# Moving one of two modulation blocks of each mixer from VectorE to TensorE in a two-layer decoder trunk

## The chip, the cores and the metric

The kernel runs on one core of one Trainium2 chip. Its engines are TensorE (PE, with its weight loads as PEld), VectorE (DVE), ScalarE (ACT), GpSimd (POOL) and SyncE (SP, which here issues most DMAs). The metric is the device time of one execution in microseconds (us), lower is better; a kernel's time is the median of its runs.

## What is computed

The reference is a trunk of two layers over 256 tokens of width 1024, in float32. Each layer has a token mixer (attention heads and RWKV-7 heads side by side) and a feed-forward part, both with adaptive modulation from one condition vector `c`:

```python
cond = jax.nn.silu(c)
for l in range(DEPTH):
    mod = cond @ w_ada[l] + b_ada[l]                       # 1024 x 6144
    sh1, sc1, gt1, sh2, sc2, gt2 = split(mod, 6)
    h = rms_norm(x, g_norm_mix[l]) * (1 + sc1) + sh1
    proj = h @ w_cat
    y_mla = mla_mixer(proj[..., :MLA_COLS], ...)           # 4 attention heads
    y_rwkv, v_first = rwkv7_mixer(token_shift(...), ...)   # 8 heads, state recurrence
    x = x + gt1 * (concat(y_mla, y_rwkv) @ w_out[l])
    h = rms_norm(x, g_norm_ffn[l]) * (1 + sc2) + sh2
    f = swiglu(...) if l % 2 == 0 else moe_swiglu(...)
    x = x + gt2 * f
return rms_norm(x, g_final)
```

The product `cond @ w_ada[l]` has one row, so each weight is used once. Its 6144 columns are cut into three blocks of 2048: block 0 holds sh1 and sc1, block 1 gt1 and sh2, block 2 sc2 and gt2.

## The kernel before

The program runs start, mixer 0, dense feed-forward 0, mixer 1, and a mixture of experts (MoE) that streams 8 experts' weights. Products that need full precision are split into high and low halves: ACT casts the high half (`split`, L187), DVE subtracts for the low one (L189), and `products` (L169) issues three matmuls per weight tile.

A mixer is written as seven threads that take turns by weights (`TUNE`, `run`): `projections` (w_in, L169 into `pp`), `prepare`, the two `recurrence` threads, `attention`, `output`, and `side`. A scheduler then sets the order on each engine, so what a thread issues lands between the instructions of the others, and each engine runs its own queue strictly in order. The recurrence inverts triangular tiles by doubling: TensorE multiplies 32x32 tiles (L716), ACT copies (`Wd`, L734), TensorE multiplies again, DVE merges (L738) and transposes (`Xd`, L743), and round again.

`side` computes blocks 1 and 2 of the layer by `ada_block`, while block 0 is done earlier (at the start for layer 0, in the feed-forward part of layer 0 for layer 1). `ada_block` loads eight weight tiles `raw` of 128x2048 from a ring of five tiles that it shares with `project` and `wout`, and has two ways to use a tile, by its argument `on_pe`:

```python
if on_pe:
    ps = ps or psp.tile([P, 512], F32, name="ada", tag="ada", bufs=1)
    for g in range(4):
        nc.tensor.matmul(ps[32 * g:32 * g + 32, :], condr[:, k, :],
                         raw[:, g * 512:(g + 1) * 512], start=k == 0, stop=k == KD - 1)
    yield
    continue
acc = acc or raw
for g in range(0, 2048, 1024):
    ...
        behind(nc.vector.tensor_scalar(acc[:, gs], raw[:, gs], ccol[:, k:k + 1], None, op0=OP.mult), first)
    ...
        nc.vector.scalar_tensor_tensor(acc[:, gs], raw[:, gs], ccol[:, k:k + 1], acc[:, gs], ...)
    yield
```

On TensorE (L233) the stationary operand is the condition repeated over 32 columns, and the four quarters of a tile go to four column groups of the array, which fill the four 32-partition parts of one PSUM bank. On DVE (L242 for the first tile, L244 for the other seven) a tile takes two instructions of 128x1024, the first tile is kept as the sum, and four matmuls with a matrix of ones (L250) add the 128 partitions at the end. Then in both ways DVE adds the bias (`ms`, L256), and four transposes (L260) and a copy (L261) put the columns into `modT`. POOL issues the load of the bias `bb` (L224), which has one buffer.

In the profile an f32 matmul counts as two instructions, so a set of four column groups is "x8".

Of the kernel before, what the change touches and what calls it, by code (L numbers as in the profile page):

```python
# [105 lines left out]
def tile_trunk(ctx: ExitStack, tc: tile.TileContext, a, out, fo, mo):  # L106
# [11 lines left out]
    def bank(name="ps", bufs=None, dt=F32):  # L118
        return psp.tile([P, 512], dt, name=name, tag="ps", bufs=bufs)
# [45 lines left out]
    def raw_tile():  # L165
        return rawp.tile([P, 2048], F32, name="raw", tag="raw")
# [12 lines left out]
    def behind(op, first):  # L179

        if first is not None:
            tc.add_manual_dep(op.ins, first.ins.name, NOSYNC, reason="order")
# [13 lines left out]
    def columns(l):  # L196
        pt = bank("pt")
        nc.tensor.transpose(pt[:, :NROWS], prow[l], ident[:NROWS, :NROWS])
        pc = cst.tile([P, NROWS], F32, name=f"par{l}")
        nc.vector.tensor_copy(pc, pt[:, :NROWS])  # L200
        par.append({k: pc[:, o:o + n] for k, (o, n) in ROWS.items()})
        omu = cst.tile([P, 15], F32, name=f"omu{l}")
        nc.vector.tensor_scalar(omu, par[l]["mu"], -1.0, 1.0, op0=OP.mult, op1=OP.add)
        oka = cst.tile([P, 4], F32, name=f"oka{l}")
        nc.vector.tensor_scalar(oka, par[l]["ka"], -1.0, 1.0, op0=OP.mult, op1=OP.add)
        par[l]["omu"], par[l]["oka"] = omu, oka
# [13 lines left out]
    def ada_block(l, blk, on_pe=False, raw_tile=raw_tile, first=None):  # L220

        ba = a["b_ada"]
        bb = mid.tile([P, 512], F32, name="bb", tag="bb", bufs=1)
        nc.gpsimd.dma_start(bb, bass.AP(tensor=ba.tensor, offset=ba.offset + l * 6 * D + blk * 2048,  # L224
                                        ap=[[512, 4], [0, 32], [1, 512]]))
        ps = acc = None
        for k in range(KD):
            raw = raw_tile()
            sync.dma_start(raw, a["w_ada"][l, k * P:(k + 1) * P, blk * 2048:(blk + 1) * 2048])
# [10 lines that stand above are left out]
                gs = slice(g, g + 1024)  # L240
                if k == 0:
                    behind(nc.vector.tensor_scalar(acc[:, gs], raw[:, gs], ccol[:, k:k + 1], None, op0=OP.mult), first)  # L242
                else:
                    nc.vector.scalar_tensor_tensor(acc[:, gs], raw[:, gs], ccol[:, k:k + 1], acc[:, gs],  # L244
                                                   op0=OP.mult, op1=OP.add)
                yield
        if not on_pe:
            ps = psp.tile([P, 512], F32, name="ada", tag="ada", bufs=1)
            for g in range(4):
                nc.tensor.matmul(ps[32 * g:32 * g + 32, :], ones[:, 0:32], acc[:, g * 512:(g + 1) * 512],  # L250
                                 start=True, stop=True)
        if (l, blk) == (1, 2):
            ms = cst.tile([P, 512], F32, name=f"ms1{blk}")
        else:
            ms = mid.tile([P, 512], F32, name="ms", tag="ms", bufs=2)
        nc.vector.tensor_add(ms, ps, bb)  # L256
        yield
        pt = bank("pt")
        for q in range(4):
            nc.tensor.transpose(pt[:, q * P:(q + 1) * P], ms[:, q * P:(q + 1) * P], ident)  # L260
        nc.vector.tensor_copy(modT[l][:, blk * 16:(blk + 1) * 16].rearrange("p (g q) -> p q g", g=4),  # L261
                              pt.rearrange("p (q n) -> p q n", q=4)[:, :, 0:P:32])
        rows[l, blk] = ms
# [128 lines left out]
    mark = {}  # L392

    def mixer(l, side, branch=()):
        pr, tune = par[l], TUNE[l]
        mp = ctx2.enter_context(tc.tile_pool(name=f"mix{l}", bufs=1, reuse_waits="tile"))
# [627 lines left out]
        def output():  # L1024
# [27 lines left out]
            for n in range(2):  # L1052
                for q, z in ((0, zh), (1, zh), (0, zl)):
                    for k in range(4):
                        mm(acc[1][n], ws[k][q][:, cs[n]], z[:, k, :], False, z is zl and k == 3, False)

        threads = dict(p=projections(), w=prepare(), r=recurrence(0), s=recurrence(1), a=attention(), o=output(), x=side(need))
        run(*[(threads[k], tune[k]) for k in tune["order"]])
        return zv["acc"], zv["gates"]


    def dense_ffn(l, side, mix):
        fd = ctx2.enter_context(tc.tile_pool(name="ffndown", bufs=1, reuse_waits="tile"))
        fp = ctx2.enter_context(tc.tile_pool(name="ffn", bufs=1, reuse_waits="tile"))
# [536 lines left out]
    for l in range(2):  # L1601
        with ExitStack() as ctx2:
            def side(need):
                yield from need(TUNE[l]["side"])
                for blk in (1, 2):
                    yield from ada_block(l, blk, first=mark.get("level4"))
                if l == 0:
                    columns(1)

            acc = mixer(l, side, acc or ())  # L1610
        with ExitStack() as ctx2:
            if l == 0:
                acc = dense_ffn(l, [(1, 0)], acc)
            else:
                midctx.close()
                moe(l, acc)
# [33 lines left out]
```

## Time and profile before

| | us |
|---|---|
| median of 3 runs | 1554.27 |
| lowest and highest run | 1550.27, 1559.34 |
| the profiled execution | 1553.52 |
| its span, first to last instruction | 1551.6 |
| PE busy | 1457.0 (94%) |
| DVE busy | 564.0 (36%) |
| ACT busy | 343.9 (22%) |
| POOL busy | 141.2 (9%) |
| mean granted TensorE clock | 0.976 |

Mixer 0 lies at about 33 to 246 us of the span and mixer 1 at about 438 to 660 us; the rest is the start, the dense feed-forward part between them, and the experts. A profile's windows give the busy time of each engine in a stretch, and the TensorE clock that was granted there as a share of 2.4 GHz. In a timeline row the two first numbers are the start and the busy time in us; what stands in brackets is the idle time of the engine before it and what ended it ("issue": nothing that the profile shows).

### The profile page before, as it was taken

Reading aid. Unit: us, or ns where it says so; the run is one execution under the profiler, and the core shown is the slowest. Engines: PE = TensorE matmul, PEld = TensorE weight load, DVE = VectorE, ACT = ScalarE, POOL = GpSimd, SP = SyncE. Lnnn points to the kernel's source line nnn. Section 1 sums busy time; section 2 is a strip of 40 time slices with the busy share of each in tenths; the row PEclk is TensorE's granted clock in tenths of the full one; section 3 lists DMA queues with packets and bytes.
Section 4 is the critical chain, followed back from the end, with each engine's and each line's share of the span. In section 5 each row is a group of like instructions: output and inputs, shape, how many; then the busy total and the mean of one; then the engine's idle time right before and its main releaser. Section 6 shows DMA issues by size and latency. Waiting matters only on the chain. (4 is left out here: it accounts for less than half of the span.)

```text
span 1551.6 us, 38224 instructions
## 1 busy us (share of the span) xinstructions
PE 1457.0 (94%) x16941; PEld 911.3 (59%) x16941; DVE 564.0 (36%) x1080; ACT 343.9 (22%) x709; POOL 141.2 (9%) x188
## 2 busy tenths in 40 slices
PE   5988998999989899999999999999999999999885
PEld 1976787999969668844535535444354454444432
DVE  1699868765567996721002002020010010000001
ACT  2823326444456243220000001000000000010001
POOL 1224100000043520100000000000000000000020
PEclk9999999999989798999999999999999999999998
DMA  9836526844545454468997999999999999999994
GB/s 321 279 116 245 184 98 242 330 188 151 181 139 178 173 209 168 149 281 329 416 414 294 415 414 412 418 413 412 418 412 388 415 413 413 415 413 417 414 411 186
DMA packets 114598, 476.51 MB, mean 307 GB/s; under 512 B 14735, under 2 KB 23707, under 8 KB 91900
## 3 DMA queue, kind: packets, MB, share of 16 engines
q1 hardware_dynamic: 111932, 469.96, 77.7%
q0 software_dynamic: 2496, 4.05, 0.9%
q8 instruction: 135, 2.21, 0.6%
q14 instruction: 35, 0.29, 0.0%
HBM read 472.92 MB, written 1.05 MB: 305 GB/s over the span
## 5 line engine op out<-in xcount | busy, mean ns | idle before, releaser
L1368 PE MATMUL up<-rawx,g 128*32 128x512 f32 (+1 forms) x2120 | 205.8, 542 | 3.5 <-DMA rawx<-in_w_exp_up_dram 3.3
L1378 DVE TENSOR_TENSOR sg<-sg,up 128x512 f32<-128x512 f32 (+1 forms) x42 | 26.1, 621 | 502.7 <-PE up L1368 501.6
L1368 PE MATMUL up<-raw,g 128*32 128x384 f32 (+1 forms) x1784 | 171.5, 537 | 1.6 <-DMA raw<-in_w_exp_up_dram 1.6
L1368 PEld LDWEIGHTS up<-rawx,g 128*32 128x32 f32 x2120 | 68.0, 110 | 135.4 <-issue 115.4
L1368 PEld LDWEIGHTS up<-raw,g 128*32 128x32 f32 x1784 | 57.5, 110 | 110.9 <-issue 100.2
L1368 PE MATMUL up<-rawt,g 128*32 128x512 f32 (+1 forms) x1120 | 109.7, 540 | 1.2 <-DMA rawt<-in_w_exp_up_dram 1.2
L189 DVE TENSOR_TENSOR wlo<-raw,whi 128x512 fp32r<-128x512 f32 x140 | 97.0, 729 | 32.4 <-PE ps L169 18.1
L1402 PE MATMUL acc<-rawx,hid 128*32 128x256 f32 x1792 | 100.2, 379 | 4.9 <-DMA rawx<-in_w_exp_down_dram 4.9
L1402 PE MATMUL acc<-raw,hid 128*32 128x256 f32 x1648 | 92.5, 380 | 2.4 <-DMA raw<-in_w_exp_down_dram 2.4
L187 ACT CAST whi<-raw 128x512 fp32r<-128x512 f32 x140 | 80.2, 624 | 59.0 <-PE ps L169 26.8
L169 PE MATMUL ps<-hh,whi 128*128 128x256 f32 x352 | 87.8, 287 | 1.8 <-ACT hh L187 1.8
L169 PE MATMUL ps<-hl,whi 128*128 128x256 f32 x352 | 87.9, 286 | 0.1
L1390 ACT COPY hid<-pt 128x512 f32<-128x512 f32 (+1 forms) x26 | 13.9, 533 | 328.8 <-PE pt L1389 328.2
L169 PE MATMUL pp<-hh,whi 128*128 128x256 f32 x296 | 80.0, 305 | 6.3 <-ACT hh L187 3.5
L1402 PEld LDWEIGHTS acc<-rawx,hid 128*32 128x32 f32 x1792 | 57.5, 110 | 45.7 <-issue 5.0
L1377 ACT ACTIVATE sg<-up 128x512 f32<-128x512 f32 (+1 forms) x42 | 22.9, 544 | 254.1 <-PE up L1368 254.1
L1443 POOL TENSOR_TENSOR fa<-fa,gate 128x512 f32<-128x512 f32 x4 | 5.1, 1281 | 814.0 <-ACT gate L272 814.0
L169 PE MATMUL pp<-hl,whi 128*128 128x256 f32 x296 | 76.8, 294 | 0.5 <-DVE hl L189 0.2
L1368 PEld LDWEIGHTS up<-rawt,g 128*32 128x32 f32 x1120 | 36.2, 110 | 68.7 <-issue 61.0
L1402 PEld LDWEIGHTS acc<-raw,hid 128*32 128x32 f32 x1648 | 52.5, 110 | 39.9 <-DMA raw<-in_w_exp_down_dram 4.3
L244 DVE SCALAR_TENSOR_TENSOR raw<-raw,ccol 128x1024 f32<-128x1024 f32 x56 | 75.0, 1359 | 0.1
L169 PEld LDWEIGHTS ps<-hh,whi 128*128 128x128 f32 x352 | 68.4, 195 | 3.7 <-ACT hh L187 2.2
(448 smaller groups left out, 2218.3 us busy)
## 6 DMA issues: line engine op xcount, KB each, us to landing
rawx<-in_w_exp_down_dram SPq DMA_DIRECT2D x43, 1024.0 KB, 17.7
raw<-in_w_ada_dram SPq DMA_DIRECT2D x40, 1024.0 KB, 5.0
raw<-in_w_exp_down_dram SPq DMA_DIRECT2D x39, 1024.0 KB, 13.3
rawx<-in_w_exp_up_dram SPq DMA_DIRECT2D x38, 1024.0 KB, 19.8
rawt<-in_w_exp_gate_dram SPq DMA_DIRECT2D x23, 1024.0 KB, 15.8
raw<-in_w_exp_gate_dram SPq DMA_DIRECT2D x30, 768.0 KB, 17.4
rawt<-in_w_exp_down_dram SPq DMA_DIRECT2D x22, 1024.0 KB, 18.4
raw<-in_w_exp_up_dram SPq DMA_DIRECT2D x21, 1024.0 KB, 16.1
```

The source lines that it names most:

```text
L169: nc.tensor.matmul(ps, w if left else x, x if left else w, start=start, stop=stop)
L187: c = nc.scalar.copy(hi, src)
L189: v = nc.vector.tensor_sub(lo, src, hi.bitcast(F32))
L244: nc.vector.scalar_tensor_tensor(acc[:, gs], raw[:, gs], ccol[:, k:k + 1], acc[:, gs], op0=OP.mult, op1=OP.add)
L1368: nc.tensor.matmul(ps[t][32 * j:32 * j + 32, :n], g[:, k, 32 * t:32 * t + 32], raw[:, j * n:(j + 1) * n], start=k == 0, stop=k == KD - 1)
L1377: nc.scalar.activation(sg, pss[0][t][:, :n], AF.Silu)
L1378: nc.vector.tensor_mul(sg, sg, pss[1][t][:, :n])
L1390: (nc.vector.tensor_copy if t == 1 else nc.scalar.copy)(hid[:, t, :nb].rearrange("p b n -> p (b n)"), pt[:, :nb * P])
L1402: nc.tensor.matmul(acc[t][32 * q:32 * q + 32, :], hid[:, t, b, 32 * j:32 * j + 32], raw[:, m % 2, 256 * q:256 * q + 256], start=s == 0 and ...
L1443: nc.gpsimd.tensor_mul(fa[:, i, cs], fa[:, i, cs], gates[n])
```

## The change

`side` now passes `on_pe` for block 1, in both layers. Block 2 stays on DVE.

```diff
             def side(need):
                 yield from need(TUNE[l]["side"])
                 for blk in (1, 2):
-                    yield from ada_block(l, blk, first=mark.get("level4"))
+                    yield from ada_block(l, blk, blk == 1, first=mark.get("level4"))
                 if l == 0:
                     columns(1)
```

The scheduler makes a new order of it. On PE in mixer 0, in the part where the attention (L885, L898) and the doubling steps (L716) alternate, the order stands thus against the one before (`ada` is the PSUM bank of the block, `condr` the repeated condition):

```order
 L885 MATMUL ps<-kpe,cf_73 128x256
 L716 MATMUL ps<-Yd,Wd 32x32 x32
+L233 MATMUL ada<-raw,condr 32x512 x4
 L898 MATMUL ps<-ukv,ckv 128x512
 L716 MATMUL ps<-Xd,LT_839 32x32 x32
+L233 MATMUL ada<-raw,condr 32x512 x4
 L898 MATMUL ps<-ukv,ckv 128x512
 L716 MATMUL ps<-Xd,LT_853 32x32 x32
+L233 MATMUL ada<-raw,condr 32x512 x4
 L651 MATMUL pt<-cf,vkeep 128x128 x8
 L661 MATMUL ps<-bv,cf_73 128x256
```

Three sets of four column groups are put in, each between a doubling step and a matmul of another thread.

A little earlier on PE, where the first doubling step of mixer 0 follows a projection:

```order
 L169 MATMUL pp<-hl,whi 128x256
 L169 MATMUL pp<-hh,wlo 128x256 x8
+L233 MATMUL ada<-raw,condr 32x512 x4
 L716 MATMUL ps<-Xd,LT_853 32x32 x32
 L169 MATMUL pp<-hh,whi 128x256
```

One set is put in ahead of the first step, which waits for DVE's `Xd`.

On DVE in mixer 1, from the merge of the second triangular tile (L727) to the next doubling step, before:

```order
L727 COPY_PREDICATED Yd<-cm,LT_5534 32x128 x4
L244 SCALAR_TENSOR_TENSOR raw<-raw,ccol 128x1024
L494 SCALAR_TENSOR_TENSOR vT<-pp,omu_2419,pm 128x256
L729 STREAM_TRANSPOSE Xd<-Yd 128x256
L887 TENSOR_TENSOR rt__5703<-sinT,ps 128x256
L244 SCALAR_TENSOR_TENSOR raw<-raw,ccol 128x1024 x2
L619 SCALAR_TENSOR_TENSOR bv<-rT,par_2417,kT 128x256 x4
L494 SCALAR_TENSOR_TENSOR vT<-pp,omu_2419,pm 128x256
L631 TENSOR_TENSOR kT<-kT,En 128x1024
L244 SCALAR_TENSOR_TENSOR raw<-raw,ccol 128x1024
L189 TENSOR_TENSOR wlo<-raw,whi 128x512 x2
L494 SCALAR_TENSOR_TENSOR vT<-pp,omu_2419,pm 128x256
```

and with the change:

```order
L727 COPY_PREDICATED Yd<-cm,LT_5558 32x128 x4
L729 STREAM_TRANSPOSE Xd<-Yd 128x256
L494 SCALAR_TENSOR_TENSOR rT<-pp,omu_2196,pm 128x256
L494 SCALAR_TENSOR_TENSOR vT<-pp,omu_2196,pm 128x256
L887 TENSOR_TENSOR rt__5735<-sinT,ps 128x256
L619 SCALAR_TENSOR_TENSOR bv<-rT,par_2194,kT 128x256 x4
L494 SCALAR_TENSOR_TENSOR vT<-pp,omu_2196,pm 128x256
L631 TENSOR_TENSOR kT<-kT,En 128x1024
L189 TENSOR_TENSOR wlo<-raw,whi 128x512 x2
L494 SCALAR_TENSOR_TENSOR vT<-pp,omu_2196,pm 128x256
```

The four L244 that stood here are gone; the low half of the last weights (`wlo`, L189) follows L631 at once.

## Rows read from the trace of the kernel before

**Rows 1.** Busy time of each engine in windows: both mixers' middles, feed-forward, mixer 0 later.

```profile
core 0: us, PE busy (x) PEld busy (x) DVE busy (x) ACT busy (x) POOL busy (x), PEclk, DMA share, GB/s
80.00:140.00 60.00, 49.06 (x897) 43.24 (x895) 56.61 (x97) 15.80 (x35) 23.43 (x23) 0.91 0.49 177
480.00:550.00 70.00, 61.39 (x746) 53.41 (x746) 67.61 (x109) 25.72 (x58) 28.72 (x31) 0.88 0.51 182
262.00:382.00 120.00, 120.00 (x850) 113.09 (x849) 77.93 (x112) 56.03 (x100) 0.00 (x0) 1.00 0.65 241
...
140.00:200.00 60.00, 55.87 (x845) 46.29 (x843) 50.38 (x111) 23.49 (x60) 12.98 (x19) 0.94 0.54 186
```

**Rows 2.** PE's waits, 80 to 140 us: us in total, times, longest.

```profile
PE ps L716 <- DVE Xd L729: 3.6, 1, 3.6
PE pt L651 <- issue: 1.9, 1, 1.9
PE ps L678 <- DVE kr L608: 1.8, 1, 1.8
PE ps L716 <- DVE Xd L743: 1.6, 1, 1.6
```

**Rows 3.** PE's waits, 480 to 550 us.

```profile
PE pp L169 <- DVE wlo L189: 3.9, 1, 3.9
PE pp L169 <- issue: 2.8, 1, 2.8
```

**Rows 4.** DVE's block products: groups by shape in 85:200 and 485:600, and source L242.

```profile
L244 DVE SCALAR_TENSOR_TENSOR raw<-raw,ccol 128x1024 f32<-128x1024 f32 x28 | 37.7, 1374 | 0.0
...
L244 DVE SCALAR_TENSOR_TENSOR raw<-raw,ccol 128x1024 f32<-128x1024 f32 x28 | 37.3, 1344 | 0.1
...
L242 DVE TENSOR_SCALAR raw<-raw,ccol x8: 711/742/1526, 81.8 to 554.5; 128x1024 f32<-128x1024 f32 x8
```

**Rows 5.** Timeline of PE around column-group matmuls: alone in the mixers.

```profile
148.04 1.06 PE L250 MATMUL ada<-raw,cf 128*32 128x512 f32 x8
149.04 0.33 PE L966 MATMUL pt<-cf,sc 128*128 128x128 f32 x1
...
562.76 1.04 PE L250 MATMUL ada<-raw,cf 128*32 128x512 f32 x2
563.74 0.70 PE L971 MATMUL ps<-PT,va 128*128 128x256 f32 x2
```

**Rows 6.** The same: eight sets in a row (MoE), and one set at the start.

```profile
689.43 7.05 PE L1368 MATMUL up<-raw,g 128*32 128x512 f32 x64
...
10.99 1.94 PE L233 MATMUL ada<-raw,condr 128*32 128x512 f32 x8 [7.52 <-DMA raw<-in_w_ada_dram]
```

**Rows 7.** Timeline of PE: the same projection step at either clock.

```profile
96.83 1.10 PE L169 MATMUL pp<-hh,wlo 128*128 128x256 f32 x8
...
531.77 2.35 PE L169 MATMUL pp<-hh,wlo 128*128 128x256 f32 x8 [3.90 <-DVE wlo L189]
```

**Rows 8.** Timeline of DVE ahead of that wait in mixer 1.

```profile
520.13 2.93 DVE L244 SCALAR_TENSOR_TENSOR raw<-raw,ccol 128x1024 f32<-128x1024 f32 x2
522.99 3.51 DVE L619 SCALAR_TENSOR_TENSOR bv<-rT,par,kT 128x256 f32<-128x256 f32 x4
...
527.95 2.19 DVE L244 SCALAR_TENSOR_TENSOR raw<-raw,ccol 128x1024 f32<-128x1024 f32 x1
530.06 2.79 DVE L189 TENSOR_TENSOR wlo<-raw,whi 128x512 fp32r<-128x512 f32 x2
```

**Rows 9.** POOL's products L630 by source, ns min/median/max, and who waited.

```profile
L630 POOL TENSOR_TENSOR ZR<-rT,Ep x8: 1269/2056/2069, 128.3 to 529.1; 64x512 f32<-64x512 f32 x8
...
  ACT va L899: 9.1, 1
```

**Rows 10.** The block's weight loads (L229), 440 to 600 us: issue to landing.

```profile
DMA to landing us min/median/max: 4.7/5.0/10.3
```

## The prediction

> **What bounds the kernel now.** I read the windows first [rows 1]. Over the whole span PE is busy 94% of the time, so the first question is whether it has any time to give. In the dense feed-forward part it has none: 120.00 of 120 us busy at clock 1.00, with DVE at 77.93 of 120, 65%. In the middles of the two mixers, where `side` runs block 1, this turns round. From 80 to 140 us DVE is busy 56.61 of 60 us (94%) and PE only 49.06; from 480 to 550 us DVE is busy 67.61 of 70 (97%) and PE 61.39. The granted clock falls there too, to 0.91 and 0.88, which means that TensorE spent part of the stretch at 1.2 GHz and not at 2.4. So DVE is the engine that decides these two stretches, and PE lies behind it.
>
> The waits of PE say the same by name: 3.6 us for the first transpose `Xd`, 1.8 for `kr` and 1.6 for a later `Xd` in mixer 0 [rows 2], 3.9 us for the low half `wlo` in mixer 1, after 2.8 that no semaphore explains [rows 3]. Behind the 3.9 the clock is low: a projection step of eight matmuls takes 2.35 us there, where it takes 1.10 at full clock [rows 7].
>
> What PE could win at most I call its room: idle time plus the part lost to the low clock. Mixer 0: 60 - 49.06 = 10.9 idle, and (1 - 0.91) x 60 = 5.4 of clock, 16.3 us. Mixer 1: 70 - 61.39 = 8.6, and 0.12 x 70 = 8.4, 17.0 us. Together 33.3 us. (The clock was also low while PE idled, so this is an upper bound.)
>
> **What leaves DVE.** Per layer 14 of the 28 L244 and two L242. In mixer 0 that is 14 x 1.374 + 2 x 0.742 = 20.7 us, in mixer 1 14 x 1.344 + 1.5 = 20.3 us [rows 4], 41 us in all. From 80 to 140 us DVE then holds some 36 of 60 us, 60%; from 480 to 550 (only the L244 lie in there, 18.8 us) 49 of 70, 70%. That is about its load in the feed-forward part, where PE had no room at all. The L244 stand in front of what PE waits for: in the 10 us ahead of `wlo` three of them take 2.93 + 2.19 us [rows 8], and the new order has L189 right behind L631.
>
> **What PE gets.** Thirty-two matmuls per layer, in sets of four column groups. A set alone between other matmuls takes 1.00 us to the start of the next (148.04 to 149.04), and one matmul alone takes nearly as much, 0.98 us, since the groups run beside each other [rows 5]; so I count the pieces into which the order cuts the sets, and not the matmuls. Mixer 0 has runs of 1, 4, 3, 4, 8, 4, 4, 4: nine sets, as the run of 8 is two. Mixer 1 has 1, 3, 1, 2, 1, 1, 3, 4, 4, 4, 4, 4: twelve. That is 21 x 1.00 = 21 us. Bounds for a set: 0.88 us, eight in a row in the experts' part (7.05 / 8), and 1.94 us at the low clock [rows 6], so 18.5 to 40.7 us; I take 1.00, as these sets stand alone and as the stretches are mostly at full clock. Of the sums with ones (L250) there were six runs and there will be four: the two halves of mixer 1 that fall away are 2 x 1.00 = 2.0 us. Net PE work: +19 us.
>
> A set alone is dearer than one of eight by 0.12 us, in all 21 x 0.12 = 2.5 us. The Trainium skill, "TensorEngine Tiling (Array Packing)", Key Properties, says that changing the tiling mode drains TensorE; that speaks against this change, and rows 5 and 6 agree with it in that size. Without such a cost the sum below would be 2.5 us lower.
>
> **What is recovered.** This is the unknown, and it lies between two rows. If the stretches become like the feed-forward part, all 33.3 us of room go: 33.3 - 19 = 14.3 us faster. If they become like mixer 0 from 140 to 200 us, with the same doubling steps and DVE at 84%, they keep 60 - 55.87 = 4.1 idle and 0.06 x 60 = 3.6 clock, 7.7 of 60, 13%: of 130 us that is 17 kept, 16.5 recovered, and 2.5 us slower. I take the middle, 6.5% kept, 8.4 us, because DVE's load will be near the feed-forward part's while the chain PE-ACT-PE-DVE of the doubling steps stays: 25 us recovered against 19 added, **6 us faster**. The places fit this. In mixer 0 a set is put into the 3.6 us idle ahead of the first doubling step, and three into the place with 1.6 and 1.9 us idle. In mixer 1 ten pieces (10 us) stand ahead of the projection that waited 2.8 + 3.9 us; they delay it by about as much as DVE's relief would have advanced it, so there the gain must come from the clock that no longer falls.
>
> **At nothing:** the bias add, transposes and copy of block 1 exist in both versions; the 16 loads per layer are the same. A tile is free after its set, and no first tile is held as the sum, so SP issues them earlier: ten of them stand ahead of mixer 0's first `w_out` load (before, seven), all 16 ahead of mixer 1's (before, 13), and one passes the last two `w_in` loads of mixer 1. With the DMA engines 49 and 51% busy in the two stretches [rows 1] I count none of this. POOL's load of `bb` for block 2 waits for the add of block 1 and has `qpe` products queued behind it; in the new order that add stands ahead of their inputs, so I expect no wait.
>
> The sum is made against the profiled execution: 1553.5 - 6 = 1547.5 us. The median of the runs shown is 0.75 us above it, so the predicted median is **1548 us**. A change of under 0.5% (7.8 us) can't be told from none.
>
> **Rivals.**
> 1. *All the room goes, and more* (0.27). For it: the feed-forward row at equal DVE load. Also a lone L244 took 2.19 us [rows 8] where the mean is 1.344, and POOL's L630 takes 1.27 us at best but 2.06 in the median, with ACT waiting 9.1 us for it once [rows 9]; if the two engines stretch each other, fewer L244 shorten both: 4 x 0.79 = 3.1 us per mixer on POOL. Block 2 ends earlier as well and may give half of the 7.7 us after 140. That is -14.3 to -18: 1536 to 1540 us. Against it: the steps need each other's results whatever DVE's load is. (The Trainium skill, "SBUF — State Buffer", SBUF: two separate sides, has DVE with two SBUF inputs and a GpSimd op that reads SBUF exclude each other for a whole instruction; by that rule this rival is the likelier, and the spread of L630 agrees.)
> 2. *PE becomes the bound* (0.17). PE's queue is in order, and a set ahead of a doubling step delays that step, then ACT, then DVE. If only 10 us of room come back (about the named waits on DVE, 3.6 + 1.8 + 1.6 + 3.9), the clock stays low where it was, and it is 19 - 10 = 9 us slower: 1563 us. It decides when under 19 us are recovered, and shows beyond the 0.5% below 11 us. For it: PE was already 82 and 88% busy.
> 3. *A weight tile comes late* (0.06). Before, a late tile stopped DVE; now a set at the head of PE's queue stops PE. Landing takes 5.0 us in the median and 10.3 at most [rows 10]; two waits of 5 us make 4 us slower, 1558 us. Against it: the loads are issued ahead, as soon as tiles come free.
>
> That the change does nothing is excluded by the order. The forecast, with 1541 to 1555 us for its own range, gets 0.50.
>
> **How the numbers follow.** Faster by over 0.5% (below 1546.5): nearly all of rival 1 (0.25) and three tenths of the forecast (0.15), 0.40. Slower by over 0.5% (above 1562): most of rival 2 and a little of rival 3, 0.15. Within: 0.45. The range for 8 of 10 goes from rival 1's lower end, 1536, to just short of rival 2, 1562.
>
> **What would show it.** Right: from 80 to 140 and 480 to 550 us DVE at 60 to 70%, clock 0.95 or more, PE's waits for `Xd` and `wlo` gone or under 1 us, L233 at about 1.0 us per set, and mixer 0 and mixer 1 each shorter by some 3 us. Wrong: the clock unchanged (rival 2), PE idle until a DMA of `w_ada` lands (rival 3), sets at 1.9 us, or a new long wait of POOL or ACT.

## The result and the profile after

The change makes the kernel slower by 8 us where I had said 6 us faster: median 1562.1 us (20 runs, 1555.7 to 1573.9) against 1554.3 us (20 runs, 1549.3 to 1560.4), ratio 1.0054, 95% interval 1.0039 to 1.0070. It lies just outside the range that I gave. The profiled execution after took 1566.46 us, span 1564.6, and another one of the same kernel 1556.28 us, so single profiles of it differ by 10 us.

The windows on which the forecast rested, after:

```profile
core 0: us, PE busy (x) PEld busy (x) DVE busy (x) ACT busy (x) POOL busy (x), PEclk, DMA share, GB/s
80.00:140.00 60.00, 56.41 (x1079) 44.02 (x1080) 39.85 (x88) 16.33 (x37) 18.78 (x23) 0.97 0.59 216
140.00:200.00 60.00, 53.02 (x663) 42.21 (x653) 38.29 (x79) 18.95 (x52) 13.49 (x18) 0.80 0.43 146
480.00:550.00 70.00, 70.00 (x746) 58.58 (x745) 48.65 (x88) 31.99 (x71) 27.91 (x34) 1.00 0.56 199
```

Against [rows 1] the two stretches that I argued from did what they should: DVE falls from 56.61 to 39.85 us and from 67.61 to 48.65, PE rises to 56.41 of 60 and to 70.00 of 70, the clock to 0.97 and 1.00. (Mixer 1 begins 15.6 us later now, so its row does not hold the same stretch of work. Over the same part, 495.6 to 565.6 us here, DVE has 52.63 of 70 us, PE 69.59 and the clock is 1.00.) The loss is in the row between them, which I had used only as a measure of what might be kept: from 140 to 200 us the clock falls from 0.94 to 0.80.

Landmarks say the same. The first L944 (scores of the first head) starts at 140.2 us (before, 141.5), so mixer 0 is 1.3 us ahead there. From here on I call what lies ahead of this L944 the first part of a mixer, and the rest the second. The warm-up matmuls L344 that end it start at 252.1 (238.0): 15.4 us are lost on the way. From the first transposes of mixer 1 (L379) to the first expert matmul (L1368) it takes 230.8 us (233.5), 2.7 us less. The second part of mixer 0, from just ahead of L944 to L344, as one window of the kernel before:

```profile
140.90:238.00 97.10, 92.97 (x1016) 77.87 (x1003) 76.67 (x167) 32.76 (x75) 13.91 (x20) 0.96 0.43 147
```

and of the changed kernel:

```profile
139.60:252.10 112.50, 103.28 (x999) 85.31 (x988) 74.50 (x163) 33.29 (x75) 14.46 (x19) 0.86 0.32 106
```

Idle time of PE goes from 97.1 - 92.97 = 4.1 to 9.2 us, and what the clock takes from 0.04 x 97.1 = 3.9 to 0.14 x 112.5 = 15.8 us. So of the 15.4 us about 5 are waits and, by this reckoning, 12 the clock at 1.2 GHz (the two overlap a little), though DVE has less to do there.

Where it begins, on PE's timeline after:

```profile
143.13 0.62 PE L716 MATMUL ps<-Yd,Wd 32*32 32x32 f32 x49 [1.07 <-issue]
...
148.99 0.69 PE L716 MATMUL ps<-Xd,LT 32*32 32x32 f32 x32 [1.55 <-DVE Xd L743]
149.61 0.55 PE L966 MATMUL pt<-cf,sc 128*128 128x128 f32 x3
151.07 1.06 PE L971 MATMUL ps<-PT,va 128*128 128x256 f32 x2 [0.91 <-ACT PT L969]
...
153.49 1.11 PE L981 MATMUL so<-cf,sq 128*128 128x64 f32 x4
154.39 2.02 PE L910 MATMUL ps<-cq,uqp 128*128 128x256 f32 x4
```

and the same place before (the L250 between the first two rows is the one of [rows 5]):

```profile
147.42 0.69 PE L716 MATMUL ps<-Xd,LT 32*32 32x32 f32 x32
...
150.23 0.70 PE L971 MATMUL ps<-PT,va 128*128 128x256 f32 x2 [0.65 <-ACT PT L969]
...
151.71 0.66 PE L260 MATMUL pt<-cf,ms 128*128 128x128 f32 x4
152.20 0.56 PE L981 MATMUL so<-cf,sq 128*128 128x64 f32 x4
152.59 1.08 PE L910 MATMUL ps<-cq,uqp 128*128 128x256 f32 x4
```

PE idles 1.07, 1.55 and 0.91 us within eight, then L910 takes 2.02 us where it took 1.08: the clock is at half and stays there to about 172 us.

```profile
150.00:160.00 10.00, 8.54 (x120) 6.25 (x118) 6.69 (x16) 3.84 (x12) 0.00 (x0) 0.56 0.83 304
160.00:170.00 10.00, 10.00 (x110) 8.37 (x110) 7.54 (x10) 1.33 (x3) 4.67 (x6) 0.50 0.61 211
```

Before, the L250 and L260 of block 1, 1.7 us of work that waits for nobody, stood in this place. Now block 1 is finished earlier (its L260 runs at 133 us), and PE has nothing else for it. DVE after, ahead of the transpose that PE waits for:

```profile
143.80 0.29 DVE L738 COPY_PREDICATED Yd<-cm,ps 128x128 f32<-128x128 uint8 x1
...
144.53 1.27 DVE L244 SCALAR_TENSOR_TENSOR raw<-raw,ccol 128x1024 f32<-128x1024 f32 x1
146.24 0.16 DVE L956 RECIPROCAL ri<-sm__1722 128x1 f32<-128x1 f32 x1 [0.44 <-ACT sc L954]
...
146.77 1.42 DVE L189 TENSOR_TENSOR wolo<-raw,wohi 128x1024 fp32r<-128x1024 f32 x1
148.11 0.43 DVE L743 STREAM_TRANSPOSE Xd<-Yd 128x256 f32<-128x256 f32 x1
```

and before:

```profile
145.25 0.28 DVE L738 COPY_PREDICATED Yd<-cm,ps 128x128 f32<-128x128 uint8 x1
...
145.96 0.43 DVE L743 STREAM_TRANSPOSE Xd<-Yd 128x256 f32<-128x256 f32 x1
146.31 0.71 DVE L242 TENSOR_SCALAR raw<-raw,ccol 128x1024 f32<-128x1024 f32 x1
```

4.3 us lie between the merge and its transpose, 0.7 before. As block 1 ends early, block 2 begins early as well: its two L242 run at 133 and 135 us, where they ran at 146 and 149, and its L244 and the low half `wolo` now stand among the doubling steps.

### The profile page after: what moved, and what is told of

It reads as the page before. It is cut to its first block, busy times and chain, and to the rows that moved or that the text cites. A ratio compares the mean times of both kernels' runs of the same rounds, so it can differ in the third digit from the quotient of the medians.

```text
span 1564.6 us, 38429 instructions
## 1 busy us (share of the span) xinstructions
PE 1476.2 (94%) x17053; PEld 914.9 (58%) x17053; DVE 524.6 (34%) x1048; ACT 343.9 (22%) x709; POOL 135.2 (9%) x188
## 5 line engine op out<-in xcount | busy, mean ns | idle before, releaser
L1368 PE MATMUL up<-rawx,g 128*32 128x512 f32 (+1 forms) x2120 | 205.7, 542 | 3.6 <-DMA rawx<-in_w_exp_up_dram 3.4
L1368 PE MATMUL up<-raw,g 128*32 128x384 f32 (+1 forms) x1784 | 171.7, 537 | 1.7 <-DMA raw<-in_w_exp_up_dram 1.6
L1368 PEld LDWEIGHTS up<-rawx,g 128*32 128x32 f32 x2120 | 68.6, 110 | 134.5 <-issue 118.2
L1368 PEld LDWEIGHTS up<-raw,g 128*32 128x32 f32 x1784 | 57.4, 110 | 111.3 <-issue 98.4
L1368 PE MATMUL up<-rawt,g 128*32 128x512 f32 (+1 forms) x1120 | 109.6, 540 | 1.2 <-DMA rawt<-in_w_exp_up_dram 1.2
L189 DVE TENSOR_TENSOR wlo<-raw,whi 128x512 fp32r<-128x512 f32 x140 | 96.6, 725 | 36.0 <-PE ps L169 19.7
L1368 PEld LDWEIGHTS up<-rawt,g 128*32 128x32 f32 x1120 | 36.2, 110 | 68.7 <-issue 61.3
L169 PEld LDWEIGHTS ps<-hl,whi 128*128 128x128 f32 x352 | 68.5, 194 | 1.4 <-DVE hl L189 0.7
## 6 DMA issues: line engine op xcount, KB each, us to landing
rawx<-in_w_exp_down_dram SPq DMA_DIRECT2D x43, 1024.0 KB, 17.6
```

Source lines behind the costliest of these rows:

```text
L169: nc.tensor.matmul(ps, w if left else x, x if left else w, start=start, stop=stop)
L189: v = nc.vector.tensor_sub(lo, src, hi.bitcast(F32))
L1368: nc.tensor.matmul(ps[t][32 * j:32 * j + 32, :n], g[:, k, 32 * t:32 * t + 32], raw[:, j * n:(j + 1) * n], start=k == 0, stop=k == KD - 1)
```

## The experiments

Theories: **A**, the new order of mixer 0 behind 140 us makes PE stall and the clock fall; **B**, the added PE work itself is the loss; **C**, the L244 of block 2 come too early on DVE. All ratios are to the kernel before, with 95% intervals; a time in us is the median of a kernel's runs.

### One layer alone

```diff
-yield from ada_block(l, blk, blk == 1, first=mark.get("level4"))
+yield from ada_block(l, blk, blk == 1 and l == 0, first=mark.get("level4"))
```

The other kernel has `l == 1`.

> Block 1 goes to TensorE in layer 0 only; mixer 1 is as before. Theory A (the new order in mixer 0 behind 140 us, where PE stalls by 0.9 to 1.6 us at a time and the granted clock then stays at 1.2 GHz for 20 us): the whole loss is here, and a little more, as mixer 1 no longer wins its 2 us: 9 to 14 us slower than before, and the low clock between 150 and 172 us again. Theory B (the added work on PE itself costs more than it frees, in either layer alike): 4 us slower, half of the loss. Theory C (block 2's L244 come earlier and stand in front of the steps): as A in time, but with PE's waits in 140 to 200 us ended by DVE with an L244 just ahead of the merge or transpose.

> Block 1 goes to TensorE in layer 1 only; mixer 0 is as before. Theory A: mixer 1 alone wins the 2 to 3 us by which the trace of the change shows it shorter, so 2 to 3 us faster than before, within what can be told from none; the wait for wlo stays away and the clock falls less in 480 to 550 us. Theory B: 4 us slower. Theory C: as A.

Layer 0 alone: 1563.9 us, 1.0070 (1.0043 to 1.0096). Layer 1 alone: 1550.8 us, 0.9980 (0.9957 to 1.0003). The loss is all in mixer 0; mixer 1 costs nothing and may win 3 us, which this interval cannot tell from none. (With layer 0 alone, mixer 1 has the instructions of before, in an order that differs in places.) Theory B's 4 us in each is out.

### Both blocks on TensorE

```diff
-yield from ada_block(l, blk, blk == 1, first=mark.get("level4"))
+yield from ada_block(l, blk, True, first=mark.get("level4"))
```

> Both blocks go to TensorE in both layers, so no L244, L242 or L250 is left in the mixers, and PE gets some 32 more sets. Theory A: what counts is the order on ACT and DVE behind 140 us; in this kernel the exps of mixer 0 (L954) stand ahead of the copies PT and oT of the previous head again, so the clock should not fall for 20 us there: mixer 0 as long as before or up to 4 us longer for its added sets, mixer 1 likewise, 0 to 8 us slower than before and not slower than the change. Theory B: twice the added work, twice the loss: 16 to 19 us slower. Theory C: without any L244 mixer 0 is shorter than before, 0 to 8 us faster.

1560.7 us, 1.0038 (1.0015 to 1.0062): neither B's 16 to 19 us nor C's gain. The second part of mixer 0 is 99.1 us long at clock 0.96 (the change, 111.9), so twice the sets do not make that loss. But here the first L944 comes at 146.8 us, 6.6 later than with the change: 12 sets run ahead of it and not 8, 4.6 us more, after 1.6 us that PE spends idle ("issue"). In this one trace the room of the first part is used up by one block, and there the added sets cost time, as B has it.

### ACT's order, and one low half on DVE

In the first, the copy PT (L969) stands behind the next head's first exp and the copy oT (L973) behind its second. In the second, `wolo` waits until the second recurrence has made its last Xd:

```diff
 for k in range(tune["early"]):
+    yield from need("xd116") if k else ()
     ws.append(wout(0, k))
...
```

> The change, but in mixer 0 the copy PT of a head stands behind the first exp of the next head on ACT and the copy oT behind its second exp, as they stand before the change; nothing else is asked of the order. Theory A with ACT's order as its cause: DVE's 7.8 us of waits for the exps (ri behind sc) go, PE's stalls at 143 to 151 us are shorter, the clock does not stay low from 150 to 172 us, and mixer 0 gives 8 to 14 us back: within 3 us of before or up to 5 us faster. If ACT's order only goes with the loss and isn't its cause, or under theories B and C: no change against the change, 6 to 10 us slower than before.

> The change, but the second low half of w_out that mixer 0 makes early (L189 wolo, 1.42 us on DVE) comes behind the transpose Xd that it stood in front of. Clock theory: PE's wait of 1.55 us for that Xd is gone or under 0.3 us, the clock falls less between 150 and 172 us, and mixer 0 gives back 5 to 10 us: 0 to 4 us slower than before. If it is the wait alone that counts, without what the clock does behind it: 1.5 us faster than the change, 7 us slower than before. If the Xd wait is not what makes the clock fall (the stall of 1.07 us ahead of it or the wait of 0.9 for PT behind it would do alone): the clock falls as before this edit and the time is that of the change, less 1 us.

1561.5 us, 1.0051 (1.0028 to 1.0074), and 1568.9 us, 1.0085 (1.0061 to 1.0109). Neither helps. With the first, DVE's waits for the exps go from 7.4 to 0.4 us (138 to 178 us), but PE waits 2.5 us for PT and 1.55 for Xd. With the second, PE's waits from 138 to 178 us are

```profile
PE ps L716 <- DVE raw L244: 2.0, 1, 2.0
PE so L981 <- ACT sq L975: 1.8, 2, 1.1
PE rhs L695 <- DVE Lak L684: 1.6, 1, 1.6
```

`wolo` is gone from the place and the wait is longer, put down to an L244 of block 2; the moved `wohi` delays sq on ACT in its turn. Here, moving one instruction only moves the stall. Why PE waited for that L244 was not tried.

### Work that nobody needs, in the stall; a stall put in; and the change once more

```diff
 pend[h] = scs
+if l == 0 and h == 1:
+    fill = psp.tile([P, 512], F32, name="ada", tag="ada", bufs=1)
+    for _ in range(3):
+        nc.tensor.matmul(fill, ones, x[:, 0, :512], start=True, stop=True)
```

> The change plus work that nothing needs: in mixer 0, behind the scores of the second head, three matmuls of 128x512 (0.59 us each) into the free bank ada, at the place where PE stood idle for 1.55 us before the doubling step on Xd. Clock theory (the stalls of 0.9 to 1.6 us there make the granted clock fall to 1.2 GHz for 20 us, and that is most of the loss of mixer 0): PE no longer idles there, the clock stays at 1.00 or falls for much less between 150 and 172 us, and the kernel is 6 to 10 us faster than the change although PE does 1.8 us more: about the time of before or up to 3 us slower. Work theory (PE is the bound and the added work is the loss): 1 to 2 us slower than the change, some 10 us slower than before.

> The kernel before, with one edit: in mixer 0 the transpose Xd of the last doubling level of the second recurrence is made six times and not once (the same values each time), which holds DVE and so PE for some 1.8 us at the place where the change stalls. Clock theory: PE idles 1 to 2 us at about 147 us, the clock falls behind it for some 10 to 20 us, and the kernel is 5 to 12 us slower than before. Without the clock: the delay itself, 1 to 2 us slower, not to be told from none.

> The change once more, for a second profile of it. If the low clock between 150 and 172 us belongs to the program, it is there again, with the same stalls ahead of it and mixer 0 some 14 us longer than before; if it was this one execution's, the stretch is at another place and the time is nearer to 1562 than to 1566 us.

The change once more: 1564.0 us, 1.0072 (1.0047 to 1.0098). Its profiled execution has the clock at 0.81, 0.50 and 0.83 in 140 to 150, 150 to 160 and 160 to 170 us, and the second part of mixer 0 is 108.4 us long. The low stretch belongs to the program; its length varies. (This execution, 1556.28 us, is among the shortest of its kernel, and its mixer 1 takes 226.6 us, 4.2 less than in the first profile.)

With the filling: 1557.0 us, 1.0027 (1.0010 to 1.0044). PE does 2.9 us more (a matmul of 128x512 takes 0.98 us there, so my 1.8 was too low), and the kernel is 5 us faster than the change; the two intervals overlap a little, but that of the change run once more lies just above. The stretch, and the window of the second part, are

```profile
146.56 2.41 PE L963 MATMUL ada<-x,cf 128*128 128x512 f32 x5 [1.19 <-issue]
148.90 0.69 PE L716 MATMUL ps<-Xd,LT 32*32 32x32 f32 x32
...
138.00:243.30 105.30, 97.76 (x1005) 79.77 (x993) 74.21 (x165) 33.36 (x75) 18.55 (x19) 0.95 0.34 114
```

The wait for Xd is gone, and the window's clock is 0.95. About half of the loss comes back, as theory A has it, and against B. The second part is 104.7 us long in this profile; the execution, 1551.75 us, was the shortest of twelve.

The kernel before with a stall (one transpose made six times): 1558.6 us, 1.0037 (1.0017 to 1.0056), 5 us slower. But the wait of PE (1.26 us) came at 165.8 us, since the second recurrence is the later one, and the clock falls behind it (0.83 from 165 to 175 us). The profiled execution, 1552.8 us, was the shortest of ten, so it does not show where the 5 us lie. It is in the direction of A and no proof.

### The last set held back

```diff
 sync.dma_start(raw, a["w_ada"][l, k * P:(k + 1) * P, blk * 2048:(blk + 1) * 2048])
+yield from hold("sc1") if hold and k == 7 else ()
 if on_pe:
...
-pend[h] = scs
+pend[h] = scs; have.add(f"sc{h}")
...
-yield from ada_block(l, blk, blk == 1, first=mark.get("level4"))
+yield from ada_block(l, blk, blk == 1, first=mark.get("level4"), hold=need if blk == 1 and l == 0 else None)
```

> The change, but in mixer 0 the eighth and last set of four column groups waits in its thread until the scores of the second head are issued, so it and what follows from it (bias, L260, block 2) stand on PE at the places that L250 and L260 of block 1 have in the kernel before, and on DVE the Xd comes ahead of the L244 and wolo again. No work is added or left out. Theory of the cover (the 1.7 us of PE work of block 1 that stood at 148 and 152 us kept PE from standing idle there, and the L244 of block 2 came too early; without them the clock falls): no wait of PE over 0.7 us from 140 to 160 us, the clock at 1.00 there, the part of mixer 0 from the first L944 to the warm-up matmuls 96 to 100 us long as in the kernel before (after the change 112 and 108), and the kernel 0 to 6 us faster than before. Work theory (the 9 added sets are the loss): no gain on the change, 8 us slower than before.

> As the one before, but the last two sets of mixer 0 wait, so one more microsecond of PE work stands at 148 to 152 us and one less ahead of 140. Theory of the cover: within 2 us of the kernel that holds one set, either way; the first part of mixer 0 is as long or up to 1 us shorter, and PE's wait of 0.6 us for PT at 150 us is partly filled. Work theory: 8 us slower than before.

1552.8 us, 0.9994 (0.9974 to 1.0014): in time the whole loss is back, with the same work. The timeline has the old order (lines are one higher, L234 is L233):

```profile
147.21 1.06 PE L234 MATMUL ada<-raw,condr 128*32 128x512 f32 x8
148.21 0.55 PE L967 MATMUL pt<-cf,sc 128*128 128x128 f32 x3
149.33 0.70 PE L972 MATMUL ps<-PT,va 128*128 128x256 f32 x2 [0.57 <-ACT PT L970]
...
150.80 0.66 PE L261 MATMUL pt<-cf,ms 128*128 128x128 f32 x4
...
138.70:238.90 100.20, 94.62 (x1009) 78.33 (x996) 74.36 (x165) 32.63 (x75) 14.03 (x20) 0.97 0.40 132
```

Clock 0.97 in the second part, 99.6 us from L944 to L344 (before, 96.4). Theory B as the cause of the loss is out: all the added sets are in this kernel. With two sets held (`k == 6`) 1556.4 us, 1.0012 (0.9997 to 1.0028), 3.6 us more in the median; there PE waits 4.7 us at 190 us for `dg` (L854 there), with one set held 2.2, before 1.7.

### The late start of block 2 alone

The held set restores two things, PE's cover and the late start of block 2 on DVE. This kernel has the second only:

```diff
 sync.dma_start(raw, a["w_ada"][l, k * P:(k + 1) * P, blk * 2048:(blk + 1) * 2048])
+yield from hold("sc1") if hold and k == 0 else ()
 if on_pe:
...
-yield from ada_block(l, blk, blk == 1, first=mark.get("level4"))
+yield from ada_block(l, blk, blk == 1, first=mark.get("level4"), hold=need if blk == 2 and l == 0 else None)
```

> The change, but in mixer 0 block 2 begins only when the scores of the second head are issued; all eight sets of block 1 stay where the change has them. So DVE has Xd ahead of L244 and wolo again and ACT the exps ahead of PT, as in the kernel that holds the last set, but PE has no work of block 1 at 148 and 152 us. Theory that block 2 came too early on DVE (its L244 in front of the transpose and of the softmax): the time of the kernel with the held set, 0 to 3 us faster or slower than before; no wait of PE for Xd over 0.5 us at 147 us and no low clock from 150 to 172 us. Theory of the cover alone (1.7 us of PE work missing at 148 and 152 us): PE stands idle there as in the change, the clock falls, 6 to 9 us slower than before. Both in part: 3 to 5 us slower.

1560.3 us, 1.0044 (1.0023 to 1.0065). In its trace the wait for Xd is gone, but not the stall:

```profile
148.81 0.70 PE L972 MATMUL ps<-PT,va 128*128 128x256 f32 x2 [1.43 <-ACT PT L970]
...
196.43 1.20 PE L855 MATMUL pb<-dg,cf 128*128 128x128 f32 x4 [4.71 <-DVE dg L854]
...
138.90:241.70 102.80, 94.85 (x1001) 78.46 (x990) 75.87 (x163) 32.12 (x73) 13.74 (x19) 0.95 0.35 116
```

PE idles 1.43 us where L250 or the held set stood (the clock is 0.83 from 150 to 160 us), and block 2, now later, delays `dg`. So the late start alone does not give the time back. How much of the loss is then the missing cover is open: the wait for `dg` is 2.5 us longer than with one set held, and that cost is this edit's own. The profiled execution, 1554.74 us, was again the shortest of twelve, 5.5 us below the median, so it does not show all of the loss. The cover alone (the filling) gave half. How the 8 us divide between the two was not separated further.

All fifteen traces agree on where the loss lies. The second part of mixer 0 takes

| layer 0 | us |
|---|---|
| block 1 on DVE (before, layer 1 alone, the stall, the two fillings of the next section) | 96.4 to 97.7 |
| the change (both profiles, layer 0 alone, ACT's order, `wolo`) | 106.8 to 111.9 |
| the change with the filling | 104.7 |
| block 2 late | 102.2 |
| one set held; two | 99.6; 104.2 |
| both blocks on TensorE | 99.1 |

### The same cure elsewhere

Unneeded matmuls at other places where PE idles and the clock is low behind it, on the kernel before and on the one with layer 1 alone (`fill(n, rhs)` issues n matmuls of 128x256 into the free bank `ada`):

```diff
+if (l, i) == (0, 0):
+    fill(5, LT[:, 0:2, :].rearrange("p h n -> p (h n)"))
 for b in LEVELS[1:]:
...
+fill(4, oT[:, MH - 1, :])
 pb = spread(ro)
```

> The kernel before with the same three pieces of unneeded work and nothing of the change. Clock theory: 4 to 10 us faster than before, since the low stretches at 100, 192 and 612 us go or shrink. Work theory: no gain, up to 6 us slower.

> Block 1 on TensorE in layer 1 only, plus work that nothing needs at three places where PE stands idle and the clock is low behind it: five matmuls of 128x256 ahead of the first doubling step of mixer 0 (idle 3.5 us, clock 0.66 from 100 to 110 us) and four ahead of the sums with dg in each mixer (idle 1.7 us at 190 us, clock 0.66 behind it, and 1.6 us in mixer 1). Clock theory: each low stretch of 6.8 us that goes gives back 3.4 us; two or three of them go, and the work lies in idle time: 4 to 9 us faster than the kernel with layer 1 alone, 8 to 12 us faster than before, about 1543 to 1547 us. Work theory: the same as with layer 1 alone or up to 4 us slower than that, 1551 to 1555 us.

The places obey. Before, 100 to 110 and 190 to 200 us have clock 0.66 each; with the filling

```profile
100.00:110.00 10.00, 10.00 (x310) 9.19 (x310) 9.93 (x21) 2.69 (x6) 1.36 (x3) 1.00 0.37 120
190.00:200.00 10.00, 9.94 (x57) 6.84 (x57) 9.33 (x28) 4.12 (x7) 0.69 (x1) 1.00 0.34 105
```

The time does not: 1552.0 us, 1.0001 (0.9974 to 1.0029) on the kernel before, and 1551.4 us, 0.9979 (0.9962 to 0.9997) with layer 1 alone, no better than without the filling (0.9980). Three such stretches gone should have been worth 4 to 10 us by my expectation, so 3.4 us for each was wrong as a price. In the second kernel's profile mixer 0 ends 2.2 us earlier than without it, and the clock is 0.74 from 560 to 580 us in mixer 1: the low stretches come and go elsewhere. This kernel has the lowest ratio of all, below the kernel before by its interval, which ends at 0.9997, and below the change, but the filling cannot be credited with it.

## Why the prediction was wrong

- **What leaves DVE:** right in the main. 36 and 49 us foretold for the two stretches, 39.85 and 48.65 measured; over the same part of mixer 1 it is 52.63, so the close hit of the second is partly luck. Of PE's waits [rows 2, 3] the first for Xd went from 3.6 to 1.8 us and not to under 1, and that for `wlo` went altogether: PE is busy 70.00 of 70, and 69.59 over the same part.
- **What PE gets:** right. The added matmuls take 9.35 us of PE in mixer 0 and 12.68 in mixer 1, 22.0 against 21 foretold, in the pieces that were counted. (One reason that I gave isn't shown: I put the 1.94 us of [rows 6] down to the low clock, but the trace has no record of the granted clock ahead of 39 us. Only the upper bound used it.)
- **What is recovered:** right in size as room, too high as time. Idle plus clock is 3.6 + 1.8 = 5.4 us in the first stretch and none in the second (0.4 over the same part), so 16.3 - 5.4 + 17.0 = 27.9 of 33.3 us came back where I took 25. Against 22 us of added work less 2.0 for L250 that would make some 8 us faster. The traces show less. The first part of mixer 1 is 108.6 to 111.0 us long in the ten of them that have block 1 alone on TensorE there, and 112.0 to 112.8 in the four that don't: about 2 us. That is near the "some 3" foretold, but the second part of mixer 1 scatters from 116 to 126 us, so the 2.7 us of the whole mixer in one profile are worth little. The first part of mixer 0, 1.3 us ahead in the profile, varies by more: from the first transposes to L944, 103.6 and 105.4 us in the two profiles of the change, and 106.4 and 104.1 in the kernel before and in the one with the stall, whose edit comes later. And where the loss is mended, with the held set, the interval of 0.9974 to 1.0014 leaves out the 0.996 of my 1548 us. So the 25 us were too many as time as well, and where the rest of the room went is open.
- **The step that failed** is the one headed "At nothing". It says that block 1's bias add, transposes and copy "exist in both versions", and it leaves 140 to 200 us unchanged. They exist in both, but before 140 us now and not at 148 and 152, and with them goes block 1's L250. I had that very L250 in [rows 5] and read only its price. It was a cover: it stood where PE would have waited for Xd and PT. Behind it block 2 moved 13 us ahead on DVE, among the doubling steps. The term that was missing is what both do to the second part of mixer 0: 15.4 us in the profiled execution, 108.4 against 96.4, some 12, in the second one, and for the whole kernel 9.6 us between the medians with layer 0 alone.
- **Rivals.** The second, "PE becomes the bound", gave 1563 us, 1 us off, for a reason that the runs refute, so that near hit is luck: it needed only 10 us to be recovered, and 28 were; with the held set the same work costs no time on the kernel before. Its sentence that the clock stays low where it was is wrong too: the clock rose there, and fell at another place. The third showed nowhere: PE waited for no load of `w_ada` in the mixers.
- **The first rival's reason** holds in part, and its time does not. L630 after:

```profile
L630 POOL TENSOR_TENSOR ZR<-rT,Ep x8: 1174/1182/2135, 125.2 to 546.7; 64x512 f32<-64x512 f32 x8
```

Its median fell from 2.06 us [rows 9] to 1.18. The mean of L244 fell from 1.37 and 1.34 us [rows 4] to 1.31 and 1.28, while its median is 1.28 in both kernels: it is a few long ones that went, among them the four of 1.7 to 1.8 us that ran beside L630 at 128 to 135 us before. The rule of the Trainium skill, "SBUF — State Buffer", SBUF: two separate sides, that DVE with two SBUF inputs and a GpSimd op that reads SBUF exclude each other, agrees in direction with that; that they do so for the whole instruction isn't shown. No gain in time can be seen from it; POOL was not what PE waited for.

## What to carry to other kernels

An instruction that waits for nobody and stands where its engine would wait is cover; before you cost its removal at its own length, look at what the engine does in its place. Under an in-order queue and a scheduler, finishing one thread's work earlier also starts that thread's next work earlier, so read the order well past the stretch that you mean to help. And hold a piece back before you give a change up: delaying the last set gave the 8 us back.

## What the runs showed of the hardware

Behind idles of 1.07, 1.55 and 0.91 us between 142 and 151 us the clock went to 1.2 GHz, and it stayed there for some 20 us although PE was then busy nearly all the time (10.00 of 10 us from 160 to 170 us at 0.50). Those matmuls took up to twice as long (L910 2.02 against 1.08 us), so here small waits cost more than their length. But taking one such stretch away need not give its price back: at 100 and 190 us it gave nothing that can be measured. And one program's executions spread by 18 us after the change, those of the kernel before by 11 beside it and by up to 17.6 in other comparisons, with the second part of mixer 0 after the change at 111.9 us in one profile and 108.4 in another: a single profile does not tell a loss of this size.

Inside a run of 64 small matmuls (L716) PE stopped after 15 of them for 0.2 to 1.1 us, with no semaphore as the reason; before, the same run is in one piece at that place. The DMA records of the traces tell what goes with it. Queue q8 loads instructions, in 135 pieces of 16 KB (packets, MB and share of the DMA engines' time, from the page after):

```profile
q8 instruction: 135, 2.21, 0.6%
```

One of them has landed at 141.76 us, and PE goes on at 143.13. In the mixers of the fifteen traces there are 110 stops of PE of 0.15 us or more that end on "issue", and every one ends 1.19 to 1.73 us behind such a landing, while the landings in mixer 0 lie 3 to 35 us apart. The 1.9 us of [rows 2] and the 2.8 of [rows 3] are among them (1.26 and 1.40 us behind). So PE very probably waits there for instructions to arrive; no run tested it. The first of the three idles ahead of the loss is of this kind, so the missing cover and block 2 do not explain it. With the held set two such stops, 0.30 and 0.70 us, stand in the same place, and the clock stays at 1.00 there.
